# Moving the last 32 prompt tokens of a sparse expert layer from the dense products to picked rows

## The chip, the core and the metric

The kernel runs on one NeuronCore of a Trainium2 chip. The metric is the device time of one execution in microseconds (us), and the number for a kernel is the median of several runs. The core has five engines with instruction streams of their own: TensorE (PE, with its weight loads shown apart as PEld), VectorE (DVE), ScalarE (ACT), GpSimd (POOL) and SyncE (SP). Each executes its stream in order. DMAs are issued from the SP, ACT and POOL streams and are moved by 16 DMA engines that all of them share.

## What is computed

One step of a decoder layer on 288 tokens (256 of a prompt, 32 of eight sample sequences) with 2048 channels. A projection feeds sparse attention and a gated causal convolution, their outputs are projected and added to the residual stream `h`, then comes the expert layer, then a gate and the last norm. The expert layer is what the change touches:

```
qh = (xc @ wq).reshape(c, PEER_HEADS, 2, PEER_HALF)
...
eidx = jnp.take_along_axis(cidx, sel, axis=-1).reshape(c, PEER_HEADS * PEER_TOPK)
g = jax.nn.softmax(best, axis=-1).reshape(c, PEER_HEADS * PEER_TOPK)
hpre = jnp.einsum('cd,ced->ce', xc, u[eidx]).astype(jnp.float32)
act = (jax.nn.gelu(hpre, approximate=False) * g).astype(xc.dtype)
return jnp.einsum('ce,ced->cd', act, v[eidx])
```

There are 16384 experts, each with one row of 2048 float32 values in `u` (`peer_u`) and one in `v` (`peer_v`). A token has 8 heads of 16 picks, so 128 experts. All inputs are float32.

## The kernel before, in words

Every large product is made of three TensorE products in the type fp32r, which takes a float32 operand in one instruction: an operand x is split into a high part (a cast on ACT, L191) and the rest (a subtraction on DVE, L192), and `tri` (L203) adds high x high, high x low and low x high in PSUM. Each of the three loads its own 128x128 weights.

The expert layer treats the two kinds of token in different ways.

**Prompt tokens, dense.** All 16384 experts are computed for the 256 prompt tokens. The experts come as 128 tiles of 128. For a tile of `u` (`u_load` L915, `u_steps` L926) eight DMAs bring 1 MB, from the SP and ACT streams in turn; DVE transposes it in 32x32 blocks (L932, two instructions of 1024 columns), it is split (`cut[0] = 2` at L819 makes each cast and subtraction two instructions of 1024 columns), 48 products with 256 moving columns follow (L941), and ACT applies gelu (L945). For `v`, `v_part` (L1064) takes groups of GRP = 4 tiles: it multiplies the activations with the gate weights (L1076), splits them, then loads four blocks of 4 tiles x 512 channels (`load_block` L209, one DMA of 1 MB each in pieces of 512 values), makes 48 products per block into four PSUM tiles, and adds each PSUM tile of 256 columns to the residual `hT` (`residual` L494, the DVE add in L496). The first LA = 25 tiles of `u` are computed ahead, in small portions given out by `look` (L958).

**The gate weights.** Which expert has which weight for a prompt token is written out as a dense matrix: for every token two one-hot 128x128 matrices are built (L1040 to L1048) and multiplied (L1050), in chunks of GCH = 32 tokens (NCH = 8 chunks), and the result goes to a DRAM buffer `Gd` (L1056), from which `v_part` reads it back.

**Sample tokens, picked.** For the 32 sample tokens only the 128 picked experts are used. The 128 partitions hold 32 tokens x 4, and a step handles one pick for each partition. `fetch` (L1123) issues one indirect DMA from POOL that brings 128 rows of 8 KB (1 MB) into the buffer `wr2`, of which there is one. For a row of `u` DVE multiplies it with the token's row and sums (L1145); for a row of `v` DVE adds it, weighted, to `acc` (L1155). Only then is the next `fetch` issued, into the same buffer. There are 32 such steps for `u` and 32 for `v`. Before the first, a prelude in the same buffer (`xs` L1133) turns the tokens' inputs by 16 TensorE transposes; at the end `acc` is copied to that buffer (`accp` L1162) and summed over the four copies by 16 products with 32 moving columns (`spl` L1166), then added to `hT`.

**Order.** The body is written in the order of the main loop at L1180: after every block of `v`, `between(u)` may emit one tile of `u` (`u_next`) and one step of the picked rows (`next(picked)`, in 9 of 16 calls). A scheduler then orders each engine's stream by that program order and by when it expects an instruction to be ready, so an instruction may go ahead of its place. The last group of `v` also makes the third norm's inputs (`gated_norm` L1112), after each block for the 4 channel tiles that are finished; it needs the picked rows' sums of the sample tokens too, as its tiles span all 288 columns.

At the start of the kernel, `conv_w` is loaded from the SP stream at L410 behind 24 loads of `w_in`, and PE transposes it (L414) ahead of the transposes that give the norm's gains (`vecs`, L341 to L343).

Of the kernel before, what the change touches and what calls it, by code (L numbers as in the profile page):

```python
# [10 lines left out]
F32 = mybir.dt.float32  # L11
F32R = mybir.dt.float32r
BF16 = mybir.dt.bfloat16
# [6 lines left out]
P = 128  # L20
D = 2048
# [28 lines left out]
GRP = 4  # L50
GCH = 32
NCH = TP // GCH
# [3 lines left out]
LK = 8  # L56
# [8 lines left out]
SIDE = 2  # L65
# [70 lines left out]
def body(ctx: ExitStack, tc: tile.TileContext, A, O):  # L136
# [66 lines left out]
    def tri(ps, a, b, first, last):  # L203
        (ah, al), (bh, bl) = a, b
        nc.tensor.matmul(ps, ah, bh, start=first, stop=False)  # L205
        nc.tensor.matmul(ps, ah, bl, start=False, stop=False)  # L206
        nc.tensor.matmul(ps, al, bh, start=False, stop=last)  # L207
# [89 lines left out]
    cnr = pa.tile([P, 1024], F32, tag="n4", name="cnr", bufs=2)[:24, :P]  # L297
# [111 lines left out]
    cwn = pa.tile([P, 1024], F32, tag="n4", name="cwn", bufs=2)[:CW]  # L409
    nc.sync.dma_start(cwn, A["conv_w"][0])  # L410
# [408 lines left out]
    cut[0] = 2  # L819
# [4 lines left out]
    eix = ff.tile([P, 2, 16], U32, tag="eix", name="eix")  # L824
    wgt = ff.tile([P, 2, 16], F32, tag="wgt", name="wgt")
    hot = ff.tile([P, 2, 16], F32, tag="hot", name="hot")
# [4 lines left out]
    pick = ab.tile([P, 3, TP], F32, tag="pick", name="pick")  # L831
# [73 lines left out]
    Ad = dram.tile([LS, P, TP], F32, tag="Ad", name="Ad")  # L905

    def reload(g):
        for t in range(GRP * g, GRP * g + GRP):
            if t < LS:
                acts[t] = ff.tile([P, T], F32, tag="ac", name=f"ar{t}", bufs=AB)[:, :TP]  # L910
                nc.scalar.dma_start(acts[t], Ad[t])
# [14 lines left out]
    def u_steps(t):  # L926
# [4 lines left out]
        for k in range(2):  # L931
            nc.vector.transpose(uT.rearrange("p (d k c b) -> p k b d c", d=ND, k=2, c=32)[:, k],  # L932
                                ur.rearrange("p (k b d r) -> p k b d r", k=2, b=2, d=ND)[:, k])
        hr, lr = split(ff, uT, D, "u8", f"u{t}", UB)
        mm = None
        for u in range(5):
            if u > 0:
                mm = mm or mm_ps(f"up{t}")
                for dt in range(4 * u - 4, 4 * u):
                    s = slice(P * dt, P * dt + P)  # L940
                    tri(mm[:, :TP], (hr[:, s], lr[:, s]), (xf[0][:, dt, :TP], xf[1][:, dt, :TP]), dt == 0, dt == ND - 1)  # L941
            if u < 4:
                yield
        ac = ff.tile([P, T], F32, tag="ac", name=f"ac{t}", bufs=AB)[:, :TP]
        nc.scalar.activation(ac, mm[:, :TP], AF.Gelu)  # L945
# [64 lines left out]
    nc.vector.tensor_tensor(out=wgt, in0=gx[:, 16:18], in1=gs[:, 16:18][:, :, None].to_broadcast([P, 2, 16]),  # L1010
                            op=ALU.mult)
    nc.vector.scalar_tensor_tensor(eix, ks_[:, 0], float(P), ks_[:, 1], op0=ALU.mult, op1=ALU.add)
    for i in range(2):
# [3 lines left out]
        nc.scalar.copy(pick[:, :, P * i:P * i + P], ps[:, :3 * P].rearrange("p (k t) -> p k t", k=3))  # L1017
# [7 lines left out]
    pib = oh.tile([P, TP], BF16, tag="pib", name="pib")  # L1025
# [31 lines left out]
    reload(0)  # L1057
    one_stack.close()
# [4 lines left out]

    def v_part(g, between):  # L1064
        last = g == NE // GRP - 1
        if g * GRP % GK == 0:
            b = g * GRP // GK
            gt = gpool.tile([P, NCH, GK, GCH], F32, tag="gt", name=f"gt{g}")
            nc.scalar.dma_start(gt[:, :NCH - 1].rearrange("p c a t -> p c (a t)"), Gd[b])
            nc.scalar.dma_start(gt[:, NCH - 1].rearrange("p a t -> p (a t)"), Gl[b // HG][b % HG])  # L1070
            gts[g * GRP // GK] = gt
        tiles = range(GRP * g, GRP * g + GRP)
        hl = []
        for t in tiles:
            v = acts[t].rearrange("p (c t) -> p c t", t=GCH)
            nc.vector.tensor_mul(v, v, gts[t // GK][:, :, t % GK])  # L1076
# [192 lines left out]
```

## Time and profile before

| | before |
|---|---|
| median of 3 runs | 2366.1 us (2356.1 to 2369.24) |
| the profiled execution | 2350.53 us, its span 2348.8 us |
| granted TensorE clock over the span | 0.976 |
| PE busy | 2238.2 us, 95% |
| DVE busy | 1937.3 us, 82% |
| ACT busy | 1043.8 us, 44% |
| POOL busy | 176.3 us, 8% |
| moved by DMA | 479.31 MB |

The span runs from the first to the last instruction of one profiled execution. Busy shares are averages over stages with different limits, so the stages have to be read one by one. A matmul's end is modelled, since matmuls are pipelined; the pace of products is read from how many of them start in a stretch that is full.

### The profile page before, as it was taken

Reading aid. Unit: us, or ns where it says so; the run is one execution under the profiler, and the core shown is the slowest. Engines: PE = TensorE matmul, PEld = TensorE weight load, DVE = VectorE, ACT = ScalarE, POOL = GpSimd, SP = SyncE. Lnnn points to the kernel's source line nnn. Section 1 sums busy time; section 2 is a strip of 40 time slices with the busy share of each in tenths; the row PEclk is TensorE's granted clock in tenths of the full one; section 3 lists DMA queues with packets and bytes.
Section 4 is the critical chain, followed back from the end, with each engine's and each line's share of the span. In section 5 each row is a group of like instructions: output and inputs, shape, how many; then the busy total and the mean of one; then the engine's idle time right before and its main releaser. Section 6 shows DMA issues by size and latency. Waiting matters only on the chain.

```text
span 2348.8 us, 44821 instructions
## 1 busy us (share of the span) xinstructions
PE 2238.2 (95%) x17715; PEld 2198.7 (94%) x17715; DVE 1937.3 (82%) x3343; ACT 1043.8 (44%) x1687; POOL 176.3 (8%) x168
## 2 busy tenths in 40 slices
PE   6999999879969979999999999999999999999997
PEld 5999989869969979999999999999999999999997
DVE  5999844569999968999998899999987787776854
ACT  3453344853358833434433443434444443334543
POOL 2033140000000000000010011111000000000000
PEclk9999989989989989999999999999999999999999
DMA  7767542468147889988989899888886666675663
GB/s 195 170 134 162 126 144 73 124 147 175 53 116 228 233 249 295 289 283 264 284 272 268 264 291 284 281 267 274 261 231 189 189 198 195 194 204 176 170 133 80
DMA packets 277569, 479.31 MB, mean 204 GB/s; under 512 B 35785, under 2 KB 99681, under 8 KB 268766
## 3 DMA queue, kind: packets, MB, share of 16 engines
q1 hardware_dynamic: 208590, 309.03, 47.3%
q10 hardware_dynamic: 56368, 93.74, 14.2%
q0 software_dynamic: 12400, 73.66, 9.3%
q8 instruction: 139, 2.28, 0.4%
q14 instruction: 72, 0.59, 0.1%
HBM read 454.17 MB, written 23.00 MB: 203 GB/s over the span
## 4 chain that ended last, share of the span: by engine, by line
PE 80%; DMA 9%; DVE 6%; ACT 3%; issue 1%; SPq 1%; ACTq 0%; DVEq 0%
PE vps L205 9%; PE vps L207 9%; PE vps L206 9%; PE up L206 8%; PE up L205 8%; PE up L207 8%; DMA ur<-in_peer_u 4%; DMA v<-in_peer_v 2%; DVE uT L932 1%; DMA Gd<-stg 1%; ACT hg L809 1%; PE gp L1050 1%; ACT at L1043 1%; ACT stg L1053 0%; PE pso L716 0%
## 5 line engine op out<-in xcount | busy, mean ns | idle before, releaser
L932 DVE STREAM_TRANSPOSE uT<-ur 128x1024 f32<-128x1024 f32 x256 | 304.6, 1222 | 88.5 <-PE up L206 71.9
L496 DVE TENSOR_TENSOR hT<-hT,vps 128x256 f32<-128x256 f32 x512 | 201.8, 410 | 39.2 <-PE vps L207 38.7
L945 ACT ACTIVATE ac<-up 128x256 f32<-128x256 f32 x128 | 49.0, 385 | 237.5 <-PE up L207 176.9
L191 ACT CAST v_3h<-v 128x1024 fp32r<-128x1024 f32 x64 | 63.9, 1047 | 121.5 <-PE vps L206 85.8
L191 ACT CAST v_0h<-v 128x1024 fp32r<-128x1024 f32 x64 | 64.0, 1047 | 114.5 <-PE vps L206 73.7
L191 ACT CAST v_2h<-v 128x1024 fp32r<-128x1024 f32 x64 | 63.9, 1047 | 97.6 <-PE vps L206 78.9
L192 DVE TENSOR_TENSOR v_3l<-v,v_3h 128x1024 fp32r<-128x1024 f32 x64 | 75.8, 1214 | 9.0 <-ACT v_3h L191 9.0
L192 DVE TENSOR_TENSOR v_0l<-v,v_0h 128x1024 fp32r<-128x1024 f32 x64 | 75.7, 1217 | 7.9 <-ACT v_0h L191 7.9
L1155 DVE SCALAR_TENSOR_TENSOR acc<-vg,hot,acc 128x2048 f32<-128x2048 f32 x31 | 72.6, 2341 | 10.1 <-DMA vg<-in_peer_v,eix 10.1
L1125 POOL DMA_INDIRECT ug<-in_peer_u,eix x32 | 37.6, 1176 | 559.2 <-DVE hot L1145 364.5
L192 DVE TENSOR_TENSOR v_1l<-v,v_1h 128x1024 fp32r<-128x1024 f32 x64 | 75.9, 1215 | 3.5 <-ACT v_1h L191 3.0
L192 DVE TENSOR_TENSOR v_2l<-v,v_2h 128x1024 fp32r<-128x1024 f32 x64 | 75.7, 1216 | 0.5 <-ACT v_2h L191 0.5
L1050 PE MATMUL gp<-at,bt 128*128 128x128 f32 x512 | 67.5, 279 | 8.3 <-ACT at L1043 6.0
L1145 DVE CUSTOM_DVE_ANT_0 ug<-ug,xr 128x2048 f32<-128x2048 f32 x32 | 72.9, 2278 | 2.4 <-DMA ug<-in_peer_u,eix 2.4
L191 ACT CAST v_1h<-v 128x1024 fp32r<-128x1024 f32 x64 | 64.0, 1047 | 21.5 <-PE vps L206 19.4
L1050 PEld LDWEIGHTS gp<-at,bt 128*128 128x128 f32 x512 | 62.5, 193 | 10.5 <-ACT at L1043 7.4
L1125 POOL DMA_INDIRECT vg<-in_peer_v,eix x32 | 43.2, 1349 | 358.2 <-DVE acc L1155 328.4
L1043 ACT ACTIVATE at<-eqa,pick 128x128 f32<-128x128 bf16 x192 | 64.2, 425 | 4.5 <-DVE eqa L1040 2.9
L463 DVE SCALAR_TENSOR_TENSOR cat<-cat,cw 128x256 f32<-128x256 f32 x120 | 52.5, 477 | 0.0
L1053 ACT COPY stg<-gp 128x256 f32<-128x256 f32 x128 | 41.8, 393 | 15.0 <-PE gp L1050 8.0
L1076 DVE TENSOR_TENSOR ac<-ac,gt 128x256 f32<-128x256 f32 x112 | 44.4, 404 | 3.1 <-ACT ac L945 3.1
L1047 DVE TENSOR_TENSOR bt<-iota,pick 128x512 f32<-128x512 f32 x64 | 43.0, 676 | 0.0
(5772 smaller groups left out, 9894.0 us busy)
## 6 DMA issues: line engine op xcount, KB each, us to landing
v<-in_peer_v SPq DMA_DIRECT2D x128, 1024.0 KB, 7.3
ur<-in_peer_u SPq DMA_DIRECT2D x512, 128.0 KB, 4.7
ur<-in_peer_u ACTq DMA_DIRECT2D x512, 128.0 KB, 4.9
Gd<-stg SPq DMA_DIRECT2D x14, 1024.0 KB
gt<-Gd ACTq DMA_DIRECT2D x32, 448.0 KB, 6.9
gl0b<-in_w_in SPq DMA_DIRECT2D x32, 128.0 KB, 4.2
gl1b<-in_w_in SPq DMA_DIRECT2D x32, 128.0 KB, 3.8
gl2b<-in_w_in SPq DMA_DIRECT2D x32, 128.0 KB, 3.8
```

The costliest lines, as they stand in the source:

```text
L191: marks["part"] = nc.scalar.copy(y, x)
L192: marks["sub"] = nc.vector.tensor_sub(z, x, y.bitcast(F32))
L205: nc.tensor.matmul(ps, ah, bh, start=first, stop=False)
L206: nc.tensor.matmul(ps, ah, bl, start=False, stop=False)
L207: nc.tensor.matmul(ps, al, bh, start=False, stop=last)
L496: nc.vector.tensor_add(x, x, ps)
L932: nc.vector.transpose(uT.rearrange("p (d k c b) -> p k b d c", d=ND, k=2, c=32)[:, k], ur.rearrange("p (k b d r) -> p k b d r", k=2, b=2, ...
L1043: nc.scalar.activation(at[:, k], eq[:, :, k], AF.Copy, scale=pick[:, 2, t0 + k:t0 + k + 1])
L1050: nc.tensor.matmul(ps[:, P * k:P * k + P], bt[:, k], at[:, k], start=True, stop=True)
L1125: nc.gpsimd.indirect_dma_start(out=gb, out_offset=None, in_=src, in_offset=bass.IndirectOffsetOnAxis(ap=eix[:, s // 16, s % 16:s % 16 + 1] ...
L1145: nc.vector.tensor_tensor_reduce(out=gb, in0=gb, in1=xr, scale=1.0, scalar=0.0, op0=ALU.mult, op1=ALU.add, accum_out=hot[:, s // 16, s % 1 ...
L1155: nc.vector.scalar_tensor_tensor(acc, gb, w, acc, op0=ALU.mult, op1=ALU.add)
```

## The change

The last 32 prompt tokens leave the dense part and are handled as a second set of picked rows, `m = 1`, after the sample tokens' set, `m = 0`. The dense products have TD = 224 moving columns, and the gate weights 7 chunks. The second set goes through the same buffer `wr2`, with a prelude and an end of its own; its indices and weights are copied from the prompt's by ACT.

With it come further edits. `v` is taken in groups of 8 tiles, by halves of 1024 channels: a block is 2 tiles x 1024 channels (`v_block`, a DMA of 1 MB in pieces of 1024 values), the sums of a half stay in four PSUM tiles over the whole group, and they are added to `hT` by four adds of 2 x 224 columns per half. Activations are weighted one tile at a time, a group ahead (`weigh`), and the gate weights are loaded earlier (`g_load`). `cut[0] = 2` is gone, so each transpose, cast and subtraction is one instruction of 2048 columns. Steps of the picked rows are given out evenly, 5 in 9 of 256 calls, each not to be issued before the last subtraction emitted so far. `gated_norm` runs after each half. `conv_w` is loaded at the start, from the ACT stream.

```diff
-GRP = 4
+GRP = 8
...
-NCH = TP // GCH
+TD = TP - TS
+NCH = TD // GCH
...
-LK = 8
+LK = 3
...
-SIDE = 2
+SIDE = 1
...
+    cwn = pa.tile([P, 1024], F32, tag="n4", name="cwn", bufs=2)[:CW]
+    nc.scalar.dma_start(cwn, A["conv_w"][0])
...
-    cut[0] = 2
...
-        for k in range(2):
-            nc.vector.transpose(uT.rearrange("p (d k c b) -> p k b d c", d=ND, k=2, c=32)[:, k],
-                                ur.rearrange("p (k b d r) -> p k b d r", k=2, b=2, d=ND)[:, k])
+        nc.vector.transpose(uT.rearrange("p (d k c b) -> p k b d c", d=ND, k=2, c=32),
+                            ur.rearrange("p (k b d r) -> p k b d r", k=2, b=2, d=ND))
...
-                    tri(mm[:, :TP], (hr[:, s], lr[:, s]), (xf[0][:, dt, :TP], xf[1][:, dt, :TP]), dt == 0, dt == ND - 1)
+                    tri(mm[:, :TD], (hr[:, s], lr[:, s]), (xf[0][:, dt, :TD], xf[1][:, dt, :TD]), dt == 0, dt == ND - 1)
...
+    def v_block(row, col, name, slot):
+        raw = raw_tile(name, slot)
+        nc.sync.dma_start(raw.rearrange("p (k c) -> p k c", k=2),
+                          A["peer_v"][0][row:row + 2 * P, col:col + 1024].rearrange("(k p) c -> p k c", k=2))
+        h, l = split(wp, raw, D, "w8", name, WB, True)
...
     def v_part(g, between):
         last = g == NE // GRP - 1
...
+        for s in range(2):
+            bank = [ax_ps(f"vps{g}_{s}{i}") for i in range(4)]
+            for b in range(GRP // 2):
+                at = v_block(P * (GRP * g + 2 * b), 1024 * s, f"v{g}_{s}{b}", b % 2)
+                for i in range(8):
+                    ps = bank[i // 2][:, TP * (i % 2):TP * (i % 2) + TD]
+                    for k in range(2):
+                        tri(ps, at(k, i), hls[GRP * g + 2 * b + k], b == 0 and k == 0 and i % 2 == 0,
+                            b == GRP // 2 - 1 and k == 1, skip_group_check=True)
+                if s == 1:
+                    for k in range(2):
+                        weigh(GRP * g + GRP + 2 * b + k)
+                if b == GRP // 2 - 1:
+                    for i in range(4):
+                        x = hT[:, 8 * s + 2 * i:8 * s + 2 * i + 2, :TD]
+                        nc.vector.tensor_add(x, x, bank[i].rearrange("p (d t) -> p d t", d=2)[:, :, :TD])
+                between(GRP // 2 * s + b)
             if last:
-                gated_norm(range(4 * u, 4 * u + 4))
+                gated_norm(range(8 * s, 8 * s + 8))
...
     def picked_steps():
...
+        for m in range(2):
+            c = slice(TP, T) if m == 0 else slice(TD, TP)
+            xs = raw_tile(f"xs{m}", 2)
...
+            for s in range(32):
+                nc.vector.tensor_tensor_reduce(out=gb, in0=gb, in1=xr, scale=1.0, scalar=0.0, op0=ALU.mult, op1=ALU.add,
+                                               accum_out=hot[:, m, s // 16, s % 16:s % 16 + 1])
+                gb = fetch(*((A["peer_u"][0], m, s + 1, f"ug{m}_{s + 1}") if s < 31 else (A["peer_v"][0], m, 0, f"vg{m}_0")))
                 yield
...
+        def take(i):
+            if i * 5 // 9 != (i - 1) * 5 // 9:
+                with tc.issue_after(marks["sub"].ins):
+                    next(picked, None)
+
+        def between(i, g=g):
+            n = GRP * g + i
+            take(2 * n)
+            u_next(n + GRP + LK + 1)
+            take(2 * n + 1)
```

## Rows read from the trace of the kernel before

**Rows 1.** The page: busy time, and busy tenths in 40 slices of the span.

```profile
PE 2238.2 (95%) x17715; PEld 2198.7 (94%) x17715; DVE 1937.3 (82%) x3343; ACT 1043.8 (44%) x1687; POOL 176.3 (8%) x168
...
PE   6999999879969979999999999999999999999997
...
DVE  5999844569999968999998899999987787776854
```

**Rows 2.** Windows: stretch, its us, busy us per engine (instructions), PEclk, DMA share, GB/s.

```profile
60.00:100.00 40.00, 40.00 (x306) 40.00 (x305) 36.72 (x58) 17.19 (x25) 0.00 (x0) 1.00 0.77 171
684.00:833.00 149.00, 142.35 (x1184) 140.31 (x1184) 134.73 (x246) 121.72 (x360) 0.00 (x0) 0.97 0.71 206
950.00:1250.00 300.00, 300.00 (x2503) 299.93 (x2503) 284.71 (x373) 122.24 (x160) 27.48 (x23) 1.00 0.88 278
1250.00:1500.00 250.00, 247.23 (x2060) 246.09 (x2059) 231.47 (x288) 99.42 (x130) 24.19 (x20) 1.00 0.90 276
1750.00:2000.00 250.00, 250.00 (x2096) 250.00 (x2095) 197.86 (x260) 102.61 (x131) 0.00 (x0) 1.00 0.68 197
```

**Rows 3.** All that the fetch line did: POOL's indirect DMAs, landing, who waited.

```profile
L1125 POOL DMA_INDIRECT ug<-in_peer_u,eix x32: 936/938/1680, 878.4 to 1279.7; - x32
L1125 POOL DMA_INDIRECT vg<-in_peer_v,eix x32: 936/1674/2014, 1289.4 to 1680.3; - x32
...
  DVE acc L1155: 10.1, 6
  DVE ug L1145: 2.4, 3
...
DMA to landing us min/median/max: 5.4/8.0/13.2
```

**Rows 4.** The page's costliest groups on DVE.

```profile
L496 DVE TENSOR_TENSOR hT<-hT,vps 128x256 f32<-128x256 f32 x512 | 201.8, 410 | 39.2 <-PE vps L207 38.7
...
L1155 DVE SCALAR_TENSOR_TENSOR acc<-vg,hot,acc 128x2048 f32<-128x2048 f32 x31 | 72.6, 2341 | 10.1 <-DMA vg<-in_peer_v,eix 10.1
...
L1145 DVE CUSTOM_DVE_ANT_0 ug<-ug,xr 128x2048 f32<-128x2048 f32 x32 | 72.9, 2278 | 2.4 <-DMA ug<-in_peer_u,eix 2.4
```

**Rows 5.** Timeline around one pick: start us, us, engine, line.

```profile
1598.99 2.34 DVE L1155 SCALAR_TENSOR_TENSOR acc<-vg,hot,acc 128x2048 f32<-128x2048 f32 x1
...
1601.61 1.68 POOL L1125 DMA_INDIRECT vg<-in_peer_v,eix  x1 [10.37 <-DVE acc L1155]
```

**Rows 6.** Tile cwn and tile vps: what sat idle until them (us, times).

```profile
  DMA cwn<-in_conv_w: 9.8, 1
...
  PE vps L342: 10.9, 1
```

**Rows 7.** Windows of the gate-weight products alone: PE, PEld, ACT.

```profile
684.00:833.00 149.00, 67.50 (x512) 62.49 (x512) 41.77 (x128) 0.97 0.71 206
```

**Rows 8.** Windows of the u products, then of the v products, alone.

```profile
833.00:2213.00 1380.00, 641.15 (x5088) 623.39 (x5088) 40.74 (x108) 0.99 0.80 245
...
833.00:2213.00 1380.00, 765.07 (x6144) 749.46 (x6144) 201.35 (x511) 0.99 0.80 245
```

**Rows 9.** PE timeline: gate-weight products; the sum over four copies, and the next.

```profile
824.42 1.95 PE L1050 MATMUL gp<-at,bt 128*128 128x128 f32 x16
...
2101.95 3.65 PE L1166 MATMUL spl<-sel,accp 128*128 128x32 f32 x32
2105.45 0.36 PE L205 MATMUL vps<-a112h,v_3h 128*128 128x256 f32 x1
```

**Rows 10.** The page's DMA queue of POOL: packets, MB, share of 16 engines' span.

```profile
q0 software_dynamic: 12400, 73.66, 9.3%
```

**Rows 11.** DVE groups by form: adds and products with PSUM, by width.

```profile
L1218 DVE TENSOR_TENSOR gate<-gate,hT 128x288 f32<-128x288 f32 x16 | 7.3, 455 | 0.4
L1227 DVE TENSOR_TENSOR yN<-yp,gB 128x512 f32<-128x512 f32 x8 | 5.2, 686 | 13.2 <-ACT sqf L1225 13.2
```

**Rows 12.** DVE timeline: 2048 columns in one instruction, and in two.

```profile
36.30 2.29 DVE L192 TENSOR_TENSOR gl0b0l<-gl0b,gl0b0h 128x2048 fp32r<-128x2048 f32 x1
...
2130.02 2.37 DVE L932 STREAM_TRANSPOSE uT<-ur 128x1024 f32<-128x1024 f32 x2 [2.27 <-PE up L206]
```

**Rows 13.** DVE timeline: the last add of a dense sum.

```profile
2213.26 0.41 DVE L496 TENSOR_TENSOR hT<-hT,vps 128x256 f32<-128x256 f32 x1
```

**Rows 14.** Tiles xs and accp: the prelude and the end of the picked set.

```profile
L1139 PE MATMUL xsp<-ident,xs x16: 270/273/328, 872.2 to 877.4; 128*128 128x128 f32 x16
...
L1133 DVE TENSOR_TENSOR xs<-xfh,xfl x1: 2292/2292/2292, 843.2 to 843.2; 128x2048 f32<-128x2048 f32 x1
...
L1162 DVE COPY accp<-acc x1: 1219/1219/1219, 1699.8 to 1699.8; 128x2048 f32<-128x2048 f32 x1
```

More of the change, by code (lines that the diff above doesn't have):

```diff
@@ L903, in body, with reload @@
     acts, gts = {}, {}
[L905 to L911, printed above, removed]
+    Ad = dram.tile([LS, P, TD], F32, tag="Ad", name="Ad")
+    def reload(t):
+        if t < LS and t not in acts:
+            acts[t] = ff.tile([P, T], F32, tag="ac", name=f"ar{t}", bufs=AB)[:, :TD]
+            nc.scalar.dma_start(acts[t], Ad[t])
     urs = {}
@@ L1016, in body @@
             nc.tensor.transpose(ps[:, P * k:P * k + P], kp_[:, i, k].rearrange("p h r -> p (h r)"), ident)
-        nc.scalar.copy(pick[:, :, P * i:P * i + P], ps[:, :3 * P].rearrange("p (k t) -> p k t", k=3))
+        n = min(P, TD - P * i)
+        nc.scalar.copy(pick[:, :, P * i:P * i + n], ps[:, :3 * P].rearrange("p (k t) -> p k t", k=3)[:, :, :n])
+    kx_ = tk.tile([P, 3, 2, 16], F32, tag="kx_", name="kx_")
+    for a in range(4):
+        nc.scalar.copy(kx_[32 * a:32 * a + 32], kp_[P - TS:, 1].rearrange("p k (g a) r -> p k g a r", a=4)[:, :, :, a])
+    nc.scalar.copy(wgt[:, 1], kx_[:, 2])
+    nc.vector.scalar_tensor_tensor(eix[:, 1], kx_[:, 0], float(P), kx_[:, 1], op0=ALU.mult, op1=ALU.add)
     look(LOOK[2])
@@ L1127, in fetch @@
         return gb
     def picked_steps():
-        xs = raw_tile("xs", 2)
-        c = slice(TP, T)
-        x4 = [x[:, :, c].bitcast(F32)[:, :, None, :].to_broadcast([P, ND, 4, TS]) for x in xf]
-        nc.vector.tensor_tensor(out=xs.rearrange("p (d a t) -> p d a t", d=ND, a=4), in0=x4[0], in1=x4[1], op=ALU.add)
-        xr = gpool.tile([P, D], F32, tag="xr", name="xr", bufs=1)
-        for u in range(4):
-            ps = ax_ps(f"xsp{u}")
-            for j in range(4):
-                dt = 4 * u + j
-                nc.tensor.transpose(ps[:, P * j:P * j + P], xs[:, P * dt:P * dt + P], ident)
-            nc.scalar.copy(xr.rearrange("p (a d r) -> p d a r", a=4, d=ND)[:, 4 * u:4 * u + 4],
-                           ps.rearrange("p (j a r) -> p j a r", j=4, a=4))
@@ L1142, in picked_steps @@
-        gb = fetch(A["peer_u"][0], 0, "ug0")
-        yield
-        for s in range(32):
-            nc.vector.tensor_tensor_reduce(out=gb, in0=gb, in1=xr, scale=1.0, scalar=0.0, op0=ALU.mult, op1=ALU.add,
-                                           accum_out=hot[:, s // 16, s % 16:s % 16 + 1])
-            gb = fetch(A["peer_u"][0], s + 1, f"ug{s + 1}") if s < 31 else fetch(A["peer_v"][0], 0, "vg0")
-            yield
-        nc.scalar.activation(hot, hot, AF.Gelu)
-        nc.vector.tensor_mul(hot, hot, wgt)
@@ L1178, in u_next @@
             nxt[0] += 1
+    for t in range(GRP):
+        weigh(t)
     for g in range(NE // GRP):
-        reload(g + 1)
         if g == NE // GRP - SIDE:
             gB = side_inputs()
-        if g == NE // GRP - 1:
             xg = wide_pair("xg")
             sq3 = ff.tile([P, T], F32, tag="ac", name="sq3", bufs=AB)
-        v_part(g, lambda u: (u_next(GRP * g + GRP + LK), next(picked, None) if (4 * g + u) * 9 // 16 != (4 * g + u - 1) * 9 // 16 else None))
+        def take(i):
[7 more added lines that the diff above has]
+            take(2 * n + 1)
+        v_part(g, between)
     gp_stack.close()
```

129 lines of the change are left out of this document (71 added, 58 removed).

## Prediction

> **What bounds the kernel now.** I read the page first [rows 1]: PE is busy 95% of the span, DVE 82%, and both rows are near 9 from slice 15 to slice 28. Averages don't say which of them sets the pace, so I read the windows next [rows 2]. The expert layer's dense part runs from about 833 us to the last dense add at 2213 us [rows 13], 1380 us or 59% of the span. In 950 to 1250 us PE is never idle, DVE is busy 284.7 of 300 us and the DMA engines 0.88; in 1750 to 2000 us, when no rows are picked any more, PE is still full but DVE falls to 198 of 250 us and DMA to 0.68. So products set the pace, and while rows are picked DVE and the DMA engines have little room.
>
> Last I read the picked rows by themselves, since the change doubles them [rows 3]. The first of 64 fetches starts at 878.4 us and the last at 1680.3 us: (1680.3 - 878.4) / 63 = 12.7 us from one to the next. There is one buffer, so a cycle is fetch, landing, DVE, next fetch, and none of it overlaps the next. Its least is the median landing of 8.0 us [rows 3], plus 2.3 us on DVE (2278 and 2341 ns) [rows 4], plus 0.28 us from DVE's end at 1601.33 to the fetch at 1601.61 [rows 5]: 10.6 us. The other 2.1 us the landed rows waited for DVE, which had other work in front; DVE itself waited for rows only 9 times of 64, 12.5 us in all [rows 3]. Before, nobody cares: the 64 cycles end some 500 us ahead of the dense part.
>
> **The change, part by part.**
>
> *Start.* PE stood 9.8 us before the transposes of conv_w, and DVE 10.9 us for the gains behind them on PE's queue [rows 6]. With conv_w issued first, both go. PE is full afterwards [rows 2]; late next is DVE's own chain to the first high parts. I take -10 us.
>
> *Gate weights.* One of 8 chunks goes. In 684 to 833 us PE is busy 142 of 149 us [rows 2], 67.5 us of it on these products [rows 7]: -67.5/8 = -8 us. The other 672 products there are for u and get cheaper by the pace below, -5 us. Two writes of 1 MB on SP's queue go too, and were not what PE waited for.
>
> *Dense products.* 5088 + 6144 = 11232 lie in the dense part [rows 8]. With 256 columns one takes 250/2096 = 119.3 ns, with 288 about 40/306 = 130.7 [rows 2]; 32 columns fewer in a straight line would be 107.9 ns. But each product loads its own weights, and 32 instructions that move only 32 columns still take (2105.45 - 2101.95)/32 = 109.4 ns each [rows 9]. No fp32r product under 256 columns is in the trace, so the bounds are 107.9 ns (-128 us), 119.3 ns (nothing, if the loads set the pace already) and, above, the rival at the end. I take 110 ns, next to the weight-load row: 11232 x 9.3 ns = -104 us of PE's work, 1236 us left of it.
>
> The Trainium skill ("TensorE: Matmul & The Clock Gate", LDWEIGHTS) puts the load of 128 columns at columns / 1.2 GHz, 107 ns, and the gap between matmuls at columns / 2.4 GHz + 2.5 ns; by these 224 columns would cost 107 ns, -142 us. The load agrees with the 109.4 ns [rows 9]; the gap doesn't, 109 ns against 119.3 ns at 256 columns.
>
> *DVE.* 512 adds of 410 ns [rows 4] become 128 of 448 columns; between 410 ns at 256 and 686 ns at 512 columns [rows 4, 11] that is some 617 ns: 202 - 79 = -123 us. The second picked set adds 73 + 74 us [rows 4] and 3.5 us for its prelude and end [rows 14]: +151 us. One instruction of 2048 columns costs 2.29 us, two of 1024 cost 2.37 [rows 12]: nothing to speak of, but a product now waits for a whole tile's cast and subtraction. While PE has tiles ready that is hidden; where a stream begins (query and gate projections) it can cost up to 1 us eight times. I take +2 us.
>
> *DMA.* The dense part has the engines busy 0.80 x 1380 = 1104 us [rows 8]. POOL's queue moved 73.66 MB in 9.3% of 2348.8 us, 338 MB per ms [rows 10]; 64 more MB (67.1 million bytes) take 199 us: 1303 us. So the dense part can't go below about 1300 us by much, whatever PE does, and at 1430 us the engines would be at 0.91, as in the windows with the landings of 8.0 us [rows 2, 3]. I therefore keep that landing.
>
> *The second set of picks.* This decides. 128 cycles one behind another now: at 10.6 us 1357 us, at 12.7 us 1630 us, where the dense part had 1380. The steps are pinned to their place among the subtractions, so a landed row should wait less for DVE, but DVE, in order, then stands before rows not yet landed, with transposes, splits and PSUM adds queued behind, and PE behind these. The landings spread from 5.4 to 13.2 us [rows 3] and DVE has about 7 us of other work per pick (198/250 [rows 2] of a tile's and a block's 96 x 119.3 ns is 9.1 us, less 1.0 for the adds, over 1.1 picks), so short landings aren't fully used. I take 11.0 us, near the lower end; ends 10.6 and 12.7.
>
> The sum, made against this execution (span 2348.8 us, 2350.5 us in all, 15.6 us under the median): first fetch 878.4 - 10 - 13 = 855; 128 x 11.0 = 1408; end of the first set and prelude of the second 20 us (about 12 at least, 2.3 us on DVE, 5.3 for the transposes, copies; up to 35, from 843.2 to 878.4 us as before [rows 14]): 2283. The last end, 1.2 us for the copy [rows 14] and 3.5 for the sums [rows 9]: 2288. From the last dense add to the end it was 2348.8 - 2213.7 = 135 us [rows 13]; the norm now has 8 channel tiles behind the last half instead of 4, +5; streams +2: a span of 2430, 2432 us in all, +81 us. On the median, some 2447; I say 2445 us. Cycles of 10.6 to 11.6 us make 2395 to 2525.
>
> **The rivals.**
>
> *Picks keep up: faster.* If landings come in at 7 us or less, a cycle is at most 9.6 us, the chain ends at 2104, and the dense part is bound by DMA and PE at some 1310 us: -70 - 23 + 7 = -86 us, 2265, on the median 2280. The point where it turns is 10.4 us a cycle, a landing of 7.8 us at once taken by DVE. For it: 5.4 us was seen, and v comes in pieces twice as long, which may ease the engines. Against it: 64 cycles of 12.7 us on average. Chance 0.36.
>
> *A wash:* a cycle of about 10.4 us, 2366. Chance 0.07.
>
> *Picks as slow as before: slower still.* 12.7 us a cycle adds 218 us: 2665. It needs DVE as full as in 950 to 1250 us all along; the work per tile without picks (198 of 250 us [rows 2]) less the adds speaks against. Chance 0.07.
>
> *Longer pieces of v hold up the picks.* Three queues share the engines. If the landing of 8.0 us against the least of 5.4 is two other queues' turns, 1.3 us each, and SP's turns get twice as long, the landing is 9.3 us and the chain 166 us longer: 2610. Nothing in rows 3 tells the queues apart, so chance 0.06. The Trainium skill ("DMA: Bandwidth & Descriptors", Queues, rings and completion order) says that each engine goes round the queues by packets of a number of descriptors, which speaks for it; no row here shows the turns.
>
> *Not one pass.* A plain float32 product of 128 columns is two instructions of 1.95/16, about 112 to 122 ns [rows 9], that is 4 passes over the columns. Should fp32r need as many under 256 columns, 224 columns cost 373 ns: 12288 products (with those of u ahead) x 254 ns = +3.1 ms. Nothing in the trace hints at it but that no such product is there. Chance 0.04.
>
> **How the numbers follow.** The forecast has 0.40, with its own range 2395 to 2525. Faster is the first rival; slower is 0.40 + 0.07 + 0.06 + 0.04 = 0.57; within 0.5%, about what can be told from no change here, 0.07. The range leaves out the last rival, the slow picks and the outer part of the fast case, where DMA too gives way: 2250 to 2625.
>
> **What would show it.** Right: the fetch line with 128 indirect DMAs over some 1400 us, about 11 us apart, the last one shortly before the last dense add; DVE waiting for ug and vg 100 us or more in all; PE idle in the dense part; a product about 110 ns where PE is full. Wrong: fetches under 10 us apart with PE full to the end (landings shorter), or a dense pace of 119 ns (weight loads) or 370 ns (passes). The conv_w wait must be gone in any case.

## The result, and the profile after

The changed kernel takes 2642.19 us (2628.44 to 2647.72, 4 runs) against 2363.88 us (2356.1 to 2369.24, 4 runs) of the kernel before beside it: a ratio of 1.1172 [1.1117, 1.1226], 278 us slower. 2445 us was forecast, in 2250 to 2625. The profiled execution took 2640.4 us, its span 2638.6 us, at a granted clock of 0.912 (0.976 before). Of the runs below, the profiled execution of e2_two_bufs alone is a slow one (2425.48 us), which its ratio leaves out.

The page of the changed kernel, busy time and slices, to be read against [rows 1], then POOL's DMA queue and costly groups (the last columns are busy us and mean ns of one, then idle us before it and what ended them), against [rows 4, 10]:

```profile
PE 2259.6 (86%) x17699; PEld 2208.1 (84%) x17699; DVE 1928.9 (73%) x2618; ACT 1000.2 (38%) x1367; POOL 361.0 (14%) x232
...
PE   7999999798898899989798970888888899984897
...
DVE  7999534699896677778688762677777788874654
...
q0 software_dynamic: 21616, 140.78, 15.5%
...
L1187 DVE SCALAR_TENSOR_TENSOR acc<-vg,hot,acc 128x2048 f32<-128x2048 f32 x62 | 145.6, 2349 | 193.0 <-DMA vg<-in_peer_v,eix 193.0
...
L1177 DVE CUSTOM_DVE_ANT_0 ug<-ug,xr 128x2048 f32<-128x2048 f32 x64 | 146.5, 2290 | 171.8 <-DMA ug<-in_peer_u,eix 162.3
...
L1198 PE MATMUL spl<-sel,accp 128*128 128x32 f32 x64 | 14.1, 402 | 99.9 <-DVE accp L1194 99.9
...
L1115 DVE TENSOR_TENSOR hT<-hT,vps 128x448 f32<-128x448 f32 x128 | 73.6, 612 | 4.8 <-PE vps L208 4.8
```

No engine is full any more where PE and DVE had been. DVE now stands before rows that have not landed for 193.0 + 162.3 = 355 us; before it was 12.5 us [rows 3]. PE stands 99.9 us before the ends of the two sets.

The windows of the changed kernel (stretch, its us, busy us per engine with instructions, granted PE clock, DMA share, GB/s), against [rows 2]:

```profile
950.00:1250.00 300.00, 275.15 (x2289) 273.26 (x2288) 233.43 (x191) 105.95 (x97) 42.49 (x23) 0.93 0.86 260
1250.00:1500.00 250.00, 212.94 (x1785) 211.95 (x1785) 191.35 (x142) 79.71 (x76) 39.79 (x20) 0.91 0.82 252
1560.00:1680.00 120.00, 41.05 (x291) 40.21 (x290) 43.37 (x25) 9.67 (x9) 15.75 (x11) 0.62 0.41 141
1750.00:2000.00 250.00, 216.28 (x1768) 213.71 (x1767) 194.05 (x152) 82.01 (x75) 53.87 (x21) 0.92 0.84 252
```

PE, DVE and the transfers all have room at once: nothing is the bound but a chain. In 1250 to 1500 us PE makes 1785 products; the kernel without picks (below) makes 2241 there, 111.6 ns each. Of the 51 us that the 456 missing products are worth, PE is idle 37 us, and the other 14 us are 1785 products at 212.94/1785 = 119.3 ns, at a mean granted clock of 0.91. What a lower clock does to the pace can be seen after a stop of PE of 3.24 us that ends at 1074.97 us: in 1079 to 1081 us the granted clock is 0.50 and products start 0.21 us apart, from 1081.05 us on 0.11 us apart. In 1560 to 1680 us, around the end of the first set, PE is idle for two thirds of the time and the mean clock falls to 0.62.

The fetch line of the changed kernel (shortest/median/longest in ns, first and last start; then who waited), against [rows 3], and the dense adds:

```profile
L1157 POOL DMA_INDIRECT ug<-in_peer_u,eix x64: 939/2747/3051, 852.7 to 2045.5; - x64
L1157 POOL DMA_INDIRECT vg<-in_peer_v,eix x64: 939/2744/3048, 1275.9 to 2426.0; - x64
...
  DVE acc L1187: 193.0, 51
  DVE ug L1177: 162.3, 50
```

```profile
L1115 DVE TENSOR_TENSOR hT<-hT,vps x12: 614/615/621, 2394.7 to 2495.1; 128x448 f32<-128x448 f32 x12
```

From one fetch to the next it is (2426.0 - 852.7)/127 = 12.39 us on average; without the 23.1 us from the last fetch of the first set to the first of the second, 12.30 us. The fetch instruction itself has become longer: its median is 2.75 us where it was 0.94 us for `u` and 1.67 us for `v`. And the last dense add comes 69 us after the last fetch.

Two windows, the first behind the end of the second set, the other ahead of the end of the first, and the first and last of six fetches around the latter (start us, us, idle before it):

```profile
2442.40:2495.70 53.30, 47.80 (x384) 46.70 (x384) 32.42 (x52) 21.88 (x32) 0.00 (x0) 0.93 0.52 138
1604.00:1645.00 41.00, 0.00 (x0) 0.00 (x0) 11.52 (x5) 0.00 (x0) 4.70 (x5) 0.50 0.37 128
```

```profile
1604.20 0.94 POOL L1157 DMA_INDIRECT vg<-in_peer_v,eix  x1 [10.10 <-DVE acc L1187]
...
1645.51 0.94 POOL L1157 DMA_INDIRECT vg<-in_peer_v,eix  x1 [7.30 <-DVE acc L1187]
```

Behind the second set's `spl` 384 products were still to be made. And the cycle isn't the same all along. From 1581.03 us on PE stands before `spl` of the first set for 73.7 us, and soon the picks are all that moves. A pick by itself then takes (1645.51 - 1604.20)/5 = 8.3 us from fetch to fetch. What a cycle takes beyond that comes with the dense part's loads and instructions beside it.

### The profile page after: what moved, and what is told of

Same layout as the page of the kernel before. It is cut to its first block, busy times and chain, and to the rows that moved or that the text cites. A ratio compares the mean times of both kernels' runs of the same rounds, so it can differ in the third digit from the quotient of the medians.

```text
span 2638.6 us, 43822 instructions
## 1 busy us (share of the span) xinstructions
PE 2259.6 (86%) x17699; PEld 2208.1 (84%) x17699; DVE 1928.9 (73%) x2618; ACT 1000.2 (38%) x1367; POOL 361.0 (14%) x232
## 5 line engine op out<-in xcount | busy, mean ns | idle before, releaser
L930 DVE STREAM_TRANSPOSE uT<-ur 128x2048 f32<-128x2048 f32 x128 | 295.2, 2307 | 10.7 <-DMA ur<-in_peer_u 9.5
L1187 DVE SCALAR_TENSOR_TENSOR acc<-vg,hot,acc 128x2048 f32<-128x2048 f32 x62 | 145.6, 2349 | 193.0 <-DMA vg<-in_peer_v,eix 193.0
L1177 DVE CUSTOM_DVE_ANT_0 ug<-ug,xr 128x2048 f32<-128x2048 f32 x64 | 146.5, 2290 | 171.8 <-DMA ug<-in_peer_u,eix 162.3
L1157 POOL DMA_INDIRECT ug<-in_peer_u,eix x64 | 141.2, 2206 | 855.8 <-DVE hot L1177 651.5
L1157 POOL DMA_INDIRECT vg<-in_peer_v,eix x64 | 124.3, 1942 | 635.1 <-DVE acc L1187 584.2
L943 ACT ACTIVATE ac<-up 128x224 f32<-128x224 f32 x128 | 45.8, 358 | 274.5 <-PE up L208 88.1
L1198 PE MATMUL spl<-sel,accp 128*128 128x32 f32 x64 | 14.1, 402 | 99.9 <-DVE accp L1194 99.9
L1115 DVE TENSOR_TENSOR hT<-hT,vps 128x448 f32<-128x448 f32 x128 | 73.6, 612 | 4.8 <-PE vps L208 4.8
L193 DVE TENSOR_TENSOR v_12l<-v,v_12h 128x2048 fp32r<-128x2048 f32 x16 | 36.6, 2287 | 6.0 <-ACT v_12h L192 6.0
L1086 DVE TENSOR_TENSOR ac<-ac,gt 128x224 f32<-128x224 f32 x112 | 40.1, 365 | 0.0
L464 DVE SCALAR_TENSOR_TENSOR cat<-glu,cw,cat 128x256 f32<-128x256 f32 x90 | 39.8, 479 | 0.0
```

What stands on the lines that cost most here:

```text
L193: marks["sub"] = nc.vector.tensor_sub(z, x, y.bitcast(F32))
L464: nc.vector.scalar_tensor_tensor(y[:, :TP], i, cw[:, ct, j:j + 1], y[:, :TP], op0=ALU.mult, op1=ALU.add)
L943: nc.scalar.activation(ac, mm[:, :TD], AF.Gelu)
L1086: nc.vector.tensor_mul(x, x, gts[t // GK][:, :, t % GK])
L1115: nc.vector.tensor_add(x, x, bank[i].rearrange("p (d t) -> p d t", d=2)[:, :, :TD])
L1157: nc.gpsimd.indirect_dma_start(out=gb, out_offset=None, in_=src, in_offset=bass.IndirectOffsetOnAxis(ap=at, axis=0))
```

## The experiments

Each ran beside the kernel before on the same chip; chips differ by half a percent, so kernels of different rounds are set against each other by the ratio. The last column is (ratio - 1) x 2364 us.

| run | sets, buffers | us | ratio to before | us to before |
|---|---|---|---|---|
| the changed kernel | 2, 1 | 2642.19 | 1.1172 [1.1117, 1.1226] | +277 |
| e1_one_set | 1, 1 | 2444.02 | 1.0400 [1.0353, 1.0446] | +95 |
| e2_two_bufs | 2, 2 | 2398.08 | 1.0163 [1.0123, 1.0202] | +39 |
| e3_cut2 | 2, 1 | 2548.83 | 1.0835 [1.0799, 1.0870] | +197 |
| e4_no_pin | 2, 1 | 2609.55 | 1.1102 [1.1056, 1.1147] | +261 |
| e5_one_set_half | 1, 1 | 2283.90 | 0.9681 [0.9646, 0.9717] | -75 |
| e6_late_spl | 2, 1 | 2599.05 | 1.1011 [1.0964, 1.1058] | +239 |
| e7_two_bufs_cut2 | 2, 2 | 2415.47 | 1.0218 [1.0172, 1.0263] | +52 |
| e8_no_picks | 0 | 2237.07 | 0.9485 [0.9454, 0.9516] | -122 |
| e9_dense_all | 1, 1 | 2360.19 | 0.9986 [0.9969, 1.0002] | -3 |
| e10_two_bufs_half_rows | 2, 2 | 2287.99 | 0.9692 [0.9665, 0.9719] | -73 |
| e11_two_bufs_short_sums | 2, 2 | 2415.40 | 1.0226 [1.0198, 1.0254] | +53 |
| e12_before_conv_w | 1, 1 | 2353.28 | 0.9969 [0.9951, 0.9986] | -7 |
| e13_gap | 2, 1 | 2648.01 | 1.1256 [1.1224, 1.1288] | +297 |
| e14_half_rows | 2, 1 | 2460.98 | 1.0458 [1.0435, 1.0482] | +108 |
| e15_gap_pinned | 2, 1 | 2694.03 | 1.1385 [1.1344, 1.1427] | +327 |

**What the dense part is worth without picks, and without the 224 columns.** e8 leaves the loop over the sets out; e9 has one set, at half as many places, and all 256 prompt tokens dense.

```
-        for m in range(2):
+        for m in range(0):
```

> The changed kernel with no picks at all: neither the sample tokens' nor the last prompt tokens' rows are fetched or summed. The bound of the dense part: if all of the loss comes from the picks, 2200 to 2260 us with TensorE at 112 ns a matmul throughout; if the dense part in its new shape is slower than before by itself, over 2300 us.

```
-TD = TP - TS
+TD = TP
...
-        for m in range(2):
+        for m in range(1):
...
-            if i * 5 // 9 != (i - 1) * 5 // 9:
+            if i * 5 // 18 != (i - 1) * 5 // 18:
```

> The changed kernel with all 256 prompt tokens in the dense products again and the picks of the sample tokens alone, at 5 of 18 places: the rest of the change without its namesake; the whole computation is done. The kernel with no picks took 2237 us, one set at this rate 47 us more; 128 x 96 matmuls at 119.3 in place of 112 ns add 90 us: 2374 us, in a range of 2345 to 2395, so nothing beside the kernel before, and the 224 columns are the only part that gains. If the rest of the change (blocks by channel halves, one addition per two channel tiles, whole instructions of 2048 columns) gains by itself, it is under 2330 us.

Windows of e8, then of e9:

```profile
1250.00:1500.00 250.00, 250.00 (x2241) 250.00 (x2241) 185.24 (x142) 105.40 (x95) 0.00 (x0) 1.00 0.70 210
```

```profile
1750.00:2000.00 250.00, 250.00 (x2109) 250.00 (x2108) 201.17 (x141) 98.91 (x88) 10.31 (x11) 1.00 0.84 248
```

Both came out as expected (e9 a little under the 2374 us that were put down, in its range). With 224 columns and no picks PE is full at 250/2241 = 111.6 ns a product, with 256 columns it is full at 250/2109 = 118.5 ns. So all of the loss is in the picks: the changed kernel stands 399 us above e8. And the rest of the change (halves, fewer adds, whole instructions, the early conv_w, the spacing in e9), taken together, neither gains nor loses: e9 is the kernel before within its interval. The 32 columns, with the chunk of gate weights that goes with them, are the one large gain, 72 us from e9 to e5.

**One set, and one set at half as many places.** With 224 columns, e5 has the last two of e9's three edits, e1 the middle one alone. The last 32 prompt tokens' sums are left out in both.

> Leaves out the second set of picked rows, so the last 32 prompt tokens get no expert sum; all else of the change stays. Chain theory (128 fetch-land-sum cycles through one buffer set the end): 64 cycles are off the path again, the dense part is bound by products and DMA, about 1290 us long, 2250 to 2300 us in all. Rival that the 224-column products, the halves of 1024 channels or the single 2048-column instructions cost the time: stays above 2500 us.

> The changed kernel with the first set of picks alone, given out half as often (at 5 of 18 places in place of 5 of 9); the prompt tokens' sums are left out. With one set at the full rate the trace showed 5523 matmuls between 860 and 1680 us, which at the 111.6 ns that it showed later take 616 us: 204 us were lost while the picks lasted. If the loss comes from picks standing in VectorE's order at places that come round faster than a pick can be fetched (some 11 us of dense work between two of them against 12.4 us a pick), then with twice the room nothing waits and the time is 2444 - 204 = 2240, at most 2290 us, and VectorE waits for rows under 30 us. If the dense part with its instructions of 2048 columns and additions per half group is itself slower, it stays at 2400 to 2450 us.

Windows of e1, while it picks and after:

```profile
1250.00:1500.00 250.00, 215.22 (x1805) 213.95 (x1804) 192.49 (x140) 83.53 (x78) 39.73 (x20) 0.92 0.81 254
...
1750.00:2000.00 250.00, 250.00 (x2241) 250.00 (x2241) 187.56 (x138) 104.33 (x92) 0.00 (x0) 1.00 0.72 212
```

The same window of e5, and who waited for its fetches:

```profile
1250.00:1500.00 250.00, 243.94 (x2157) 242.69 (x2156) 203.86 (x162) 98.60 (x93) 22.73 (x12) 0.99 0.86 255
```

```profile
  DVE ug L1177: 46.0, 12
  DVE acc L1187: 10.0, 4
```

e1 missed: half the picks should have ended early and cost little, but it is still 95 us slower than before. Its windows say why. While it picks it is as slow as the changed kernel (1805 products against 1785), afterwards as fast as e8. e5 has the same 64 picks of one buffer and differs by the number of places alone, and it is 170 us faster. A place comes round every 1.8 calls of 48 products, 1.8 x 48 x 111.6 ns = 9.6 us of dense work. A pick's cycle is 12.4 us. DVE takes its instructions in order, so at each place it stands until the row is there, and the dense part marches at the pace of the picks. With 19.3 us between places a row is mostly there in time, and one set costs 47 us over e8. It is the spacing of the places against the cycle that decides, not the number of picks. Part of the 170 us comes at the set's end: in e1 PE stands 72.6 us before `spl`, in e5 not at all.

**Two buffers.** The next fetch is issued one pick ahead, into a second buffer; room for it comes from one activation buffer and one gate-weight buffer.

```
-AB = 12
+AB = 11
...
-        gb = raw_tile(name, 2)
+        gb = raw_tile(name, 2) if fetched[0] % 2 else gpool.tile([P, D], F32, tag="gb2", name=name, bufs=1)
...
-            gb = fetch(A["peer_u"][0], m, 0, f"ug{m}_0")
+            ahead_ = [fetch(A["peer_u"][0], m, s, f"ug{m}_{s}") for s in range(2)]
```

> The changed kernel with two buffers for picked rows, so that one fetch is under way while DVE sums the row before (room made by one buffer less for activations, 11 for 12, and one instead of two for gate weights). Chain theory: the cycle falls from 12.4 us to what DVE and DMA allow, 9 to 10 us, DVE's waits for rows fall from 355 us to under 120 us, 2300 to 2400 us. Rival that DVE's stream is overfull or badly ordered: no gain, 2600 us or more.

```profile
1250.00:1500.00 250.00, 237.67 (x2073) 236.52 (x2072) 220.19 (x152) 94.78 (x87) 41.78 (x24) 0.98 0.97 289
1560.00:1680.00 120.00, 111.83 (x967) 110.19 (x966) 106.95 (x90) 47.53 (x42) 15.09 (x12) 0.99 1.00 287
```

At the upper end of the range: 238 us of the 277 go when a row is fetched while the one before is summed, and DVE's waits for rows fall from 355 to 55 us. But it isn't faster than before, and now the DMA engines are at 0.97 and 1.00. Two runs ask what holds it there. e10 fetches 4 KB into the first half of the buffer and has DVE read that half twice; e11 fetches whole rows and sums 64 of 2048 elements. Each has one of its two sums here, the other is cut in the same way.

```
-                nc.vector.tensor_tensor_reduce(out=gb, in0=gb, in1=xr,
+                nc.vector.tensor_tensor_reduce(out=xr.rearrange("p (k c) -> p k c", k=2), in0=gb[:, None, :1024].to_broadcast([P, 2, 1024]), in1=xr.rearrange("p (k c) -> p k c", k=2),
...
```

> The changed kernel with two pick buffers, each pick fetching 4 KB in place of 8 KB a row, while VectorE's instructions keep their 2048 elements (they read the half twice); leaves out half of each picked row. With whole rows it took 2398 us, 161 us over the kernel with no picks, at a DMA share of 0.94 to 1.00. If the transfers bound it, half of the picks' 134 MB gives back about half of that: 2310 to 2345 us. If it is VectorE's work and the order on it, it stays at 2370 to 2400 us.

```
-                nc.vector.tensor_tensor_reduce(out=gb, in0=gb, in1=xr,
+                nc.vector.tensor_tensor_reduce(out=gb[:, :64], in0=gb[:, :64], in1=xr[:, :64],
...
```

> The changed kernel with two pick buffers and whole rows fetched, but VectorE multiplies and sums only the first 64 elements of each; leaves out the rest of each picked row's sums. If the transfers bound the kernel with two buffers, it stays at 2370 to 2400 us. If VectorE's 126 instructions of 2.3 us are what its dense work has no room for, some 277 us of its work are gone and it comes near the kernel with no picks: 2240 to 2300 us.

The same window of e10, then of e11:

```profile
1250.00:1500.00 250.00, 247.53 (x2215) 247.16 (x2214) 234.79 (x173) 103.36 (x97) 41.03 (x25) 1.00 0.86 253
```

```profile
1250.00:1500.00 250.00, 233.73 (x2007) 231.44 (x2006) 170.14 (x150) 89.86 (x85) 34.87 (x23) 0.96 0.97 281
```

They part DVE's work from the transfers. With 250 us less work on DVE (1676.7 us in all, 1927.0 us in e2) nothing is gained (DVE 170 of 250 us, DMA still 0.97). With 67 MB less to move 112 us go, more than expected, and PE is full although DVE works 235 of 250 us; e10 has e2's smaller buffers for activations and gate weights, so these aren't what held e2. So behind the chain stands a second limit: two sets of picks bring 134 MB into a stage whose DMA engines are at 0.70 without any. e7 (the edits of e2 and of e3, below, together) belongs here:

> The changed kernel with two pick buffers and with the transposes and splits in two instructions of 1024 columns again. Two buffers alone gave 2398 us with 55 us of VectorE's waits for rows left, the two instructions alone 93 us less than the changed kernel. If what is left with two buffers is still the pick cycle, shorter fetch instructions take most of those 55 us: 2345 to 2375 us. If it is bound by the transfers (0.95 of the DMA engines' time) or by VectorE's own work, which the cut makes longer, it stays at 2385 to 2430 us.

It fell into its second bracket, as a kernel bound by transfers should; the bracket itself would also hold DVE's work, which e11 speaks against.

**What makes the cycle long.** e3 puts back the two instructions of 1024 columns for every transpose, cast and subtraction (and the layouts that go with them).

```
+    cut[0] = 2
...
-        nc.vector.transpose(uT.rearrange("p (d k c b) -> p k b d c", d=ND, k=2, c=32),
-                            ur.rearrange("p (k b d r) -> p k b d r", k=2, b=2, d=ND))
+        for k in range(2):
+            nc.vector.transpose(uT.rearrange("p (d k c b) -> p k b d c", d=ND, k=2, c=32)[:, k],
+                                ur.rearrange("p (k b d r) -> p k b d r", k=2, b=2, d=ND)[:, k])
```

> The changed kernel with transposes, casts and subtractions in two instructions of 1024 columns again, as in the kernel before. If the fetch instruction on POOL takes 2.07 us instead of 1.26 on average because it waits for the end of a long DVE instruction: fetches come down to about 1.3 us, the cycle by 0.8 us, 2530 to 2560 us. If the length of DVE's instructions has no part in it: 2640 us, within 1%.

Its fetch line:

```profile
L1159 POOL DMA_INDIRECT ug<-in_peer_u,eix x64: 936/1678/1982, 860.3 to 1976.0; - x64
L1159 POOL DMA_INDIRECT vg<-in_peer_v,eix x64: 936/1045/1980, 1252.1 to 2332.8; - x64
...
DMA to landing us min/median/max: 5.2/8.2/14.0
```

As expected: a cycle of (2332.8 - 860.3)/127 = 11.59 us (11.50 us without the hand-over between the sets), shorter fetches (medians of 1.68 and 1.05 us), and 80 us less by the ratios. The timeline of the changed kernel shows how an instruction of DVE gets into a fetch of POOL. Three fetches, and what DVE did beside each (start us, us, engine, line):

```profile
1088.37 0.94 POOL L1157 DMA_INDIRECT ug<-in_peer_u,eix  x1 [13.26 <-DVE hot L1177]
...
1114.29 2.75 POOL L1157 DMA_INDIRECT ug<-in_peer_u,eix  x1 [11.57 <-DVE hot L1177]
1126.80 0.94 POOL L1157 DMA_INDIRECT ug<-in_peer_u,eix  x1 [9.77 <-DVE hot L1177]
```

```profile
1088.01 2.31 DVE L930 STREAM_TRANSPOSE uT<-ur 128x2048 f32<-128x2048 f32 x1
...
1113.93 2.29 DVE L193 TENSOR_TENSOR u38l<-uT,u38h 128x2048 fp32r<-128x2048 f32 x1
...
1126.44 1.68 DVE L1115 TENSOR_TENSOR hT<-hT,vps 128x448 f32<-128x448 f32 x3
```

Beside the subtraction of two SBUF tiles the fetch takes 2.75 us and ends at 1117.04 us, 0.8 us after the subtraction (1113.93 + 2.29 = 1116.22). Beside a transpose of the same length, which reads one SBUF tile, and beside adds whose second operand is in PSUM, it takes 0.94 us. It is so throughout: 77 of the 128 fetches begin beside such a subtraction of 2048 columns, take 2.74 to 3.05 us and end 0.81 to 0.82 us after it. The Trainium skill ("SBUF — State Buffer", Who interferes with whom) has the rule: a VectorE instruction with two SBUF inputs and a GpSimd instruction that reads SBUF share a read interface, and the one that starts first keeps it to its end. The trace agrees with it at these places. The same section of the Trainium skill tells of a probe in which `tensor_tensor` did not stall a DMA; here this subtraction, a `tensor_tensor`, held up the instruction of an indirect DMA, which reads its row numbers (`eix`) from SBUF, by 1.8 us, and the measurement decides. The change made the subtractions twice as long, and so this wait.

e13 and e15 were to price it alone, by a short maximum over one SBUF operand on DVE behind each pick. In e13, which has the second line below without the first, the scheduler moved it elsewhere and fetches still began beside subtractions, so its question wasn't asked (67 fetches are still over 2.7 us long); it shows only that 94 us more of DVE's work cost about 1%, 20 us by the ratios. e15 fixed the order, also for the subtractions traced after it.

```
+        with tc.issue_after(i.ins):
+            marks["gap"] = nc.vector.tensor_reduce(rd, xf[0][:, 0:2].bitcast(F32), axis=AX.X, op=ALU.max)
```

> The changed kernel with one short maximum over 576 SBUF columns on VectorE right behind each pick, so that the next fetch starts beside an instruction that reads one SBUF operand and not beside a subtraction that reads two. In the changed kernel 77 of 128 fetches lasted 2.75 us, each ending 0.81 us after such a subtraction ended, and those that began beside a transpose of the same length 0.94 us. If two-operand instructions hold the fetch up, all fetches take 0.94 us, the mean falls from 2.07 by 1.1 us, the cycle from 12.4 to about 11.3 us and the time to 2480 to 2560 us, although VectorE does some 85 us more work. If only the length of VectorE's instructions matters, or the fetch is not what the cycle waits for, it stays at 2620 us or above.

> The run before last again, with the order made sure: the short maximum over one SBUF operand stands right behind each pick on VectorE and ahead of every subtraction traced after it (in the earlier run it had drifted elsewhere, so fetches still began beside subtractions, 2.75 to 3.05 us long, and 94 us more of VectorE's work cost nothing). If two-operand instructions hold the fetch up, nearly all fetches take 0.94 us, the mean falls from 2.07 by about 1.1 us, and the time to 2480 to 2560 us. If it is any instruction of VectorE's, or the fetch is not what the cycle waits for, 2600 us or above.

The fetch line of e15, and DVE's two longest waits:

```profile
L1161 POOL DMA_INDIRECT ug<-in_peer_u,eix x64: 934/936/977, 854.3 to 2031.4; - x64
L1161 POOL DMA_INDIRECT vg<-in_peer_v,eix x64: 936/936/1784, 1227.9 to 2456.8; - x64
```

```profile
DVE ac L1090 <- ACT ac L947: 111.5, 34, 5.7
DVE ug L1185 <- DMA ug<-in_peer_u,eix: 78.5, 33, 9.8
```

What makes a fetch long is confirmed: with a one-operand instruction beside them, nearly all are short. What it costs is not: DVE's waits for rows fall to 98 us, but in the pinned order DVE stands 111.5 us before activations that ACT hasn't finished, and the time rises, into the second bracket. The packets of POOL's queue in the traces, 144 to a fetch, tell where a cycle goes (means in us, without the hand-over):

| | before | changed | e3 | e15 |
|---|---|---|---|---|
| the fetch instruction | 1.26 | 2.09 | 1.43 | 0.94 |
| its start to the first packet | 2.53 | 3.83 | 2.76 | 1.94 |
| its start to the end of the last packet | 7.35 | 8.51 | 7.77 | 6.43 |
| from there to DVE's start | 2.79 | 1.21 | 1.14 | 3.47 |
| DVE, and on to the next fetch | 2.59 | 2.59 | 2.59 | 2.59 |
| cycle | 12.73 | 12.30 | 11.50 | 12.49 |

In e3, 0.74 of the 0.80 us that the cycle is shorter lie ahead of the last packet, where the fetch stands. In e15 the row is in 2.1 us sooner and waits 2.3 us longer for DVE. So e3 gives the price, some 80 us, with the reserve that it shortens casts and transposes too.

Part of the rest of the cycle is transfer. e14 is the changed kernel with the edit of e10, one buffer as it was:

> The changed kernel with its one pick buffer, each pick fetching 4 KB in place of 8 KB a row, VectorE's work as it is; leaves out half of each picked row. If the landing (7.7 to 8.5 us) is the transfer of 1 MB beside the other queues' loads, it falls by 2 to 3 us, the cycle to about 10 us and the time to 2330 to 2430 us. If most of it is fixed time from issue to landing that the bytes don't set, the cycle stays over 11.5 us and the time over 2540 us.

Its fetches run from 846.8 to 2248.8 us, a cycle of 11.04 us, and it is 169 us faster by the ratios. It lies between the two brackets: 4 KB less a row are worth 1.35 us of 12.39, not 2 to 3. How much of the landing is fixed time isn't shown.

**Two suspects that weren't it, or half.** e4 takes the steps' pin away, e6 gives the first set's end a place six calls later.

```
-                with tc.issue_after(marks["sub"].ins):
-                    next(picked, None)
+                next(picked, None)
```

> The changed kernel without the pin of the picked steps behind the last subtraction. Chain theory: the cycles are the same number and about as long, so 2560 to 2720 us. Rival that the pinned order makes DVE stand before rows not yet landed: faster by 4% or more, under 2530 us, with DVE's waits for rows mostly gone.

```
             nc.vector.tensor_copy(turn(at), lanes(acc))
+            for _ in range(6 if m == 0 else 0):
+                yield
```

> The changed kernel with the matmuls of the first set's end (spl) put six places further back, so that TensorE meets them after VectorE has got there. If the chain of picks sets the pace, TensorE's 74 us in front of them were slack that it waits out elsewhere, and the time stays within 1.5% of the changed kernel, 2605 to 2680 us. If that block is a cost of its own, it falls by 50 to 75 us, to 2565 to 2590 us.

The pin is worth 17 us by the ratios, with an uncertainty of about as much. The end of the first set lands between its two brackets: 38 us less, about half of PE's wait of 74 us before `spl`. In 1560 to 1680 us PE is now busy 80 us instead of 41; that the chain takes back the rest is likely, but not shown.

**conv_w alone,** loaded at the start from the ACT stream, in the kernel before:

```
-    nc.sync.dma_start(cwn, A["conv_w"][0])
+    nc.scalar.dma_start(cwn, A["conv_w"][0])
```

> The kernel before with conv_w loaded early on ScalarE's queue, as in the changed kernel, and nothing else. The prediction's term: TensorE's wait of 9.8 us goes, 8 to 12 us less, a ratio of 0.995 to 0.9965. If what stands behind that wait is late as well, no change, 0.998 to 1.002.

7 us less, between 3 and 12: a little under the first bracket, and clear of the second. It is the only complete kernel here that is faster than both.

## Why the prediction was right or wrong

It had the sign and the chain of picks right, and was 197 us short: two of its steps failed, the fetch and landing within a cycle and the end of the dense part. Its sum against the span:

| part of the span | predicted us | measured us |
|---|---|---|
| start to the first fetch | 855 | 852.7 |
| first to last fetch | 1417 | 1573.3 |
| last fetch to the end of the last dense add | 16 | 69.7 |
| from there to the end | 142 | 142.9 |
| span | 2430 | 2638.6 |

- *Start, gate weights, tail.* Right: the first fetch comes 2 us from where it was put, the tail 1 us. That the first is so near is luck in part: in e5 and e14, alike up to there, it starts at 842.9 and 846.8 us. conv_w was put at -10 us and measured at -7 in e12.
- *Dense products, "I take 110 ns".* Near: 111.6 ns in e8. At 32 columns less a product fell by 7 ns, not by 11, so the weight-load row [rows 9] was the one to be near; the whole was put at -117 us (-104, and -8 and -5 in the gate weights' stretch) and is 72 us from e9 to e5. The gap formula that the prediction takes from the Trainium skill ("TensorE: Matmul & The Clock Gate") is given there, under Back-to-back issue gap, for an isolated matmul and has no part for the weight load. Here, with a load for each product, 256 columns took 118.5 ns (e9) against its 109.
- *DVE's adds.* Right: 612 ns, 617 forecast.
- *"One instruction of 2048 columns costs 2.29 us ... nothing to speak of."* The first step that failed, with the next. The sum weighed what these instructions cost DVE, and not what stands beside them: a fetch that starts beside a subtraction waits it out, and the fetch instruction grew from 1.26 to 2.09 us on average. The rows were there: fetches of 936 and of 1674 ns on one line [rows 3]. Undoing it gave back 0.8 us a cycle and 80 us of the whole (e3).
- *"I therefore keep that landing", "I take 11.0 us."* 12.30 us measured; with the hand-over, which took 23.1 us where some 31 were put, that is 156 us more than forecast. Landed rows do wait less for DVE, 1.21 us after the last packet instead of 2.79, by nearly as much as was assumed. But the landing isn't kept: the last packet comes 1.16 us later than before. All of that lies ahead of the first packet (3.83 us instead of 2.53); from the first to the last it takes 4.68 us, 4.82 before. 0.8 us of the 1.3 went with e3's cut. Of the other 0.5 us, 0.4 are landing too (7.77 us in e3 against 7.35); why stays open.
- *The sum let the dense part end with the picks.* The second step that failed, 53 us. The steps have places among the dense calls (the last pick's is at call 231 of 256, 128 x 9/5), so what stands behind the last in an engine's order can't be done in the waits before. In the trace PE stands 26.2 us before `spl` of the second set, and 384 products, 8 calls' worth, come behind it in 2442.4 to 2495.7 us. The prediction said that DVE "stands before rows not yet landed" and then added up the chain as if dense work ran freely beside it. e1 and e5 show the same from the other side.
- *"Picks keep up", 2280 us, chance 0.36.* Not only the landing stood against it. Even with the serial chain gone (e2) it is 2398 us, since transfers are at 0.97 and 1.00 in the windows shown; only with half the bytes (e10) does the kernel reach 2288. "The dense part can't go below about 1300 us" was too low: this rival took 1310 us for it, and with two buffers (e2) the last dense add is at 2281.2 us, 1448 us behind 833 us, in the profiled execution.
- *"Picks as slow as before: slower still"*, 12.7 us and 2665 us, chance 0.07, came nearest, by luck: its reason, rows that wait for a full DVE, didn't come (1.21 us instead of 2.79, DVE at 233 of 300 us), and the longer landing took its place. *Longer pieces of v*, 2610 us, wasn't tried by itself, and its number is near as well; but the packets of a row take no longer than before from the first to the last, so its mechanism isn't seen. *Not one pass* is out: a product takes 111.6 ns.

## What to carry to other kernels

A step that waits for its own transfer and has a place in an in-order engine costs little only while the dense work between two places is longer than its cycle (47 us for 64 steps in e5, 217 us in e1); compare these two numbers, and not the sums of the two chains. Moving work from products to gathered rows moves it to the transfers: here 32 columns gave back 72 us, and 67 MB of rows cost more than that with one buffer and with two. Before making an engine's instructions longer, look at what has to start beside them.

## What was not expected of the hardware

The instruction of an indirect DMA on POOL took 0.94 us or up to 3.05 us, by what DVE was doing when it began: a two-operand instruction in SBUF holds it, a transpose or an add from PSUM does not. And DVE can be very full without harm: in e10 it works 294.53 of 300 us while PE makes its 2687 products without an idle moment:

```profile
950.00:1250.00 300.00, 300.00 (x2687) 299.88 (x2687) 294.53 (x244) 121.86 (x115) 66.37 (x38) 1.00 0.88 270
```
